# Gathering six experts' rows while the last two compute, and placing the last two's rows by one-hot products

## The chip, the cores and the metric

The kernel runs on one core of a Trainium2 chip. The metric is device time in microseconds (us) of one execution, the median of several runs. A TensorE clock of 1.0 in the profile is 2.4 GHz, one of 0.5 is 1.2 GHz.

The engines are named as in the profile: PE (matrix products; PEld is its weight load), DVE (VectorE), ACT (ScalarE), POOL (GpSimd), SP (issues most DMAs). A name with a q behind it (PEldq, DVEq, SPq) is an engine's instruction queue.

## The reference, cut to what matters

A two-layer network over 512 image tokens and 256 context tokens, width 1024. Each layer is a token mixer (two linear-attention scans) and a channel mixer, each followed by a layer norm. The second layer's channel mixer is a mixture of eight experts, of which each token uses two; behind it comes the last layer norm, whose output is the kernel's.

```python
def _moe_swiglu(h, router_w, router_b, w_gate_up, w_down):
    logits = (h @ router_w) + router_b
    top_val, top_idx = lax.top_k(logits, 2)
    combine = ... softmax(top_val) put at top_idx ...       # [512, 8]
    out = 0
    for e in range(8):
        gate, up = split(h @ w_gate_up[e], 2)               # 1024 x 2816
        out += combine[:, e] * ((silu(gate) * up) @ w_down[e])   # 1408 x 1024
# last layer, then the output:
x = _layer_norm(ALPHA * x + mod_x[:, 5] * f_x, ln_g[1, 1], ln_b[1, 1])
```

All inputs are float32; weights and activations are split in two parts (high and low, `wh`/`wl`), and a product is three matmuls (high by high, high by low, low by high).

## The kernel before

All that the change touches is the mixture of experts of the second layer (`moe_open`, `router_open`, `moe`), the last quarter of the run.

**Routing.** The experts are sorted by how many tokens chose them: rank 0 has the most. Rank r has room for `CAP[r]` tokens (256, 192, 192, 128, 128, 128, 64, 64). What does not fit goes to overflow blocks, computed in a loop after the streams (`For_i`, L1497) that runs as often as a table (`tabi`) says; in the profiled execution TensorE does no product in it. For each rank `index` finds the tokens in its slots (`ix`), and `gather_x` fetches their rows from DRAM with an indirect DMA on POOL.

**Streams.** Two streams run side by side, their steps interleaved by a cost table: ranks 0, 1, 2 and ranks 6, 3, 7, 4, 5 (`STREAMS`). Per expert 17.3 MB of weights are read by SP's DMAs in pieces of 0.5 MB into five raw buffers (`wr`), copied by ACT (`wh`, L134 and L149), subtracted by DVE (`wl`, L135 and L150), and multiplied on PE. So the last expert of the one stream is rank 2 (192 tokens, computed as 128 and 64) and that of the other rank 5 (128 tokens). At the third step of a stream's last expert `ahead` loads what the end needs: the residual rows `xr` (512 x 1024) and the norm's gain and bias `gb`.

**Rows back to tokens.** An expert's finished rows (`y`, weighted on DVE, L1434 and L1436) are written by SP to a DRAM table `ysd` with one row for each slot, plus 5 x 128 rows for overflow that are set to zero early (L1093). After the overflow loop POOL issues eight indirect DMAs (L1534) that read, for each of four tiles of 128 tokens and each of a token's two choices, the row at index `sidx` and add it to `xr[t]` while it lands.

**The end.** For each tile: moments on DVE (L833, L840), an inverse square root on POOL (L843), the affine on ACT (L1545), gain and bias on DVE and POOL (L1546, L1547), and the write of the output (L1548).

What sets the order: the code is written in program order, and a scheduler places each engine's instructions; the loop at L1497 is a barrier that nothing is moved across.

Of the kernel before, what the change touches and what calls it, by code (L numbers as in the profile page):

```python
# [7 lines left out]
F32 = mybir.dt.float32  # L8
F32R = mybir.dt.float32r
# [40 lines left out]
class Kern:  # L50
# [386 lines left out]
    def small(self, tag, n, parts=P, bufs=1):  # L437
        return self.sp.tile([parts, n], F32, tag=tag, name=self.nm(tag), bufs=bufs)
# [617 lines left out]
    def moe_open(self):  # L1056
        nc, I, tc = self.nc, self.I, self.tc
        self.rk_cm = tc.tile_pool(name="rk", bufs=1, side="right")
        rp = self.rp = self.rk_cm.__enter__()
        keep = lambda shape, tag, dt=F32: rp.tile([P] + list(shape), dt, name=tag)  # L1060
        self.xhd = tc.dram_tile([TX, D], F32, name="xhd")
        self.ysd = tc.dram_tile([NSLOT + NOVB * P, D], F32, name="ysd")
        self.bc5 = keep([D], "bc5")

        self.iota1 = keep([256], "iota1")
        nc.gpsimd.iota(self.iota1, pattern=[[1, 256]], base=1, channel_multiplier=0, allow_small_or_imprecise_dtypes=True)
        i8 = self.iota8
        self.caprow, self.ltm = keep([8], "caprow"), keep([8, 8], "ltm")
        for r in range(8):
            nc.gpsimd.memset(self.caprow[:, r:r + 1], float(CAP[r]))  # L1070
        nc.vector.tensor_tensor(self.ltm, i8[:, None, :].to_broadcast([P, 8, 8]), i8[:, :, None].to_broadcast([P, 8, 8]), OP.is_lt)
# [12 lines left out]
        self.rb = keep([N_E], "rb")  # L1084
        b = I["router_b"][0]
        nc.sync.dma_start(self.rb, bass.AP(tensor=b.tensor, offset=b.offset, ap=[[0, P], [1, N_E]]))

    def router_open(self):
        nc, lp = self.nc, self.lp
        zt = lp.tile([P, D], F32, name="zt")  # L1090
        nc.gpsimd.memset(zt, 0.0)
        for b in range(NOVB):
            nc.sync.dma_start(self.ysd[NSLOT + b * P:NSLOT + (b + 1) * P], zt)  # L1093
        self.full = lp.tile([P, KT, TX], F32, name="hfull")
        self.plog = self.psum("tr", [P, NX, N_E])

# [7 lines left out]
    def moe(self, l, aff):  # L1104
# [67 lines left out]
        def index(r, late=None):  # L1172

            for b in range((CAP[r] + P - 1) // P):
# [92 lines left out]
        nc.vector.tensor_tensor(c88, c88, bc(caprow), OP.mult)  # L1267
# [26 lines left out]
        nc.vector.tensor_tensor(sl, inc, bt(base), OP.add)  # L1294
        nc.vector.tensor_scalar(sl, sl, 1.0, None, op0=OP.subtract)

        alt = small([NX, 8], "alt")
        nc.vector.tensor_scalar(alt, ovp, float(NSLOT - 1), None, op0=OP.add)
        nc.vector.tensor_tensor(alt, alt, sl, OP.subtract)
# [139 lines left out]
        def rank_gen(r, xs, big):  # L1439
            e = bass.ds(nc.sync.value_load(expi[0:1, r:r + 1], min_val=0, max_val=7), 1)  # L1440
            gs = lambda i, j, c0, n: wgu[:, e, i:j, c0:c0 + n].rearrange("p e k c -> p (e k) c")
            ds_ = lambda a, n: wdn[:, e, a:a + n, :].rearrange("p e a c -> p (e a) c")
            off = sum(CAP[:r])

            def write(m, c, y):
                nc.sync.dma_start(ysd[off + m * P:off + m * P + y.shape[0], c], y)
            return expert(CAP[r], xs, gs, ds_, "accA" if big else "accB", write, lambda m: wsl[r, m])

        xr, gb = [], []

        def ahead(big):

# [28 lines left out]
        done, wait = [0, 0], None  # L1481
# [14 lines left out]
        novb = nc.values_load(tabi[0:1, 0:1], min_val=0, max_val=NOVB)  # L1496
        with tc.For_i(0, novb) as iv:  # L1497
            ev = nc.sync.value_load(tabi[0:1, bass.ds(iv + 1, 1)], min_val=0, max_val=7)
            o_h = mg.tile([P, NX, P], F32R, tag="gat", name="ovoh", bufs=3)
# [18 lines left out]
            xs, parts = gather_x(P, [ix])  # L1518
# [5 lines left out]
            ysv = ysd[NSLOT:, :].rearrange("(b p) c -> b p c", p=P)  # L1524

            def write(m, c, y):
                nc.sync.dma_start(ysv[bass.ds(iv, 1), :, c].rearrange("b p c -> (b p) c"), y)
            for _ in expert(P, xs, gs, ds_, "accB", write, lambda m: ow):
                pass


        for u in range(0, NX, 2):
            for j, t in itertools.product(range(2), (u, u + 1)):
                nc.gpsimd.indirect_dma_start(out=xr[t], out_offset=None, in_=ysd[:, :],  # L1534
                                             in_offset=bass.IndirectOffsetOnAxis(ap=sidx[:, j, t:t + 1].bitcast(mybir.dt.uint32), axis=0),
                                             compute_op=OP.add)
# [12 lines left out]
        fin_cm.__exit__(None, None, None)  # L1549
        mp_cm.__exit__(None, None, None)  # L1550
# [80 lines left out]
```

## Time and profile before

| | us |
|---|---|
| median of 3 runs | 2245.61 (2241.24 to 2247.71) |
| the profiled execution | 2239.29 |
| its span in the trace | 2237.4 |
| PE busy | 2063.8 (92%) |
| DVE busy | 1467.1 (66%) |
| POOL busy | 204.1 (9%) |
| last product of PE ends, from the span's start | 2189.8 |

The span is what the trace shows from the first to the last instruction; the execution's own time is 1.9 us longer. "Idle before, <- X" behind an instruction says how long its engine stood idle before it, and what ended the wait. Instructions that only wait, branch or issue DMAs are not counted as busy.

### The profile page before, as it was taken

How to read it: one execution, taken by the hardware profiler on the slowest of the kernel's cores; microseconds unless marked ns; L12 is line 12 of the kernel's file. 1: busy time of each engine (PE TensorE's matmuls, PEld its weight loads, DVE VectorE, ACT ScalarE, POOL GpSimd, SP SyncE). 2: the span in 40 equal slices, each digit the busy share in tenths (PEclk: the TensorE clock that was granted, in tenths of full speed). 3: DMA queues.
4: the chain of work that ended last, by engine and by line, in shares of the span. 5: the costliest groups of instructions: out<-in, count | busy, mean ns of one | idle time of the engine just before them, and what ended most of it. 6: DMA issues, size and time to landing. Idle time of an engine off the chain costs nothing. (4 is left out here: it accounts for less than half of the span.)

```text
span 2237.4 us, 31754 instructions
## 1 busy us (share of the span) xinstructions
PE 2063.8 (92%) x12273; PEld 1746.0 (78%) x12273; DVE 1467.1 (66%) x2519; ACT 891.3 (40%) x1411; POOL 204.1 (9%) x185
## 2 busy tenths in 40 slices
PE   8999699999999999999999999999768998889991
PEld 3887588986888888888888888898767787677771
DVE  4466584825787755555555677785688768677774
ACT  3346232323442222211224354334147656666661
POOL 1001101000200000022000011102510000000003
PEclk9999799999999999999999999999769999899995
DMA  7123112136454433322131221216278879788875
GB/s 257 48 82 109 37 36 83 46 139 221 156 185 148 157 132 132 132 76 76 60 120 44 81 71 43 67 57 211 101 229 283 257 262 309 236 278 294 287 268 129
DMA packets 233475, 332.29 MB, mean 149 GB/s; under 512 B 13936, under 2 KB 181044, under 8 KB 233320
## 3 DMA queue, kind: packets, MB, share of 16 engines
q1 hardware_dynamic: 229624, 318.09, 43.4%
q0 software_dynamic: 3696, 12.13, 2.1%
q8 instruction: 98, 1.61, 0.3%
q14 instruction: 57, 0.47, 0.1%
HBM read 305.98 MB, written 24.19 MB: 148 GB/s over the span
## 5 line engine op out<-in xcount | busy, mean ns | idle before, releaser
L165 PE MATMUL g<-xh,wh 128*128 128x512 f32 (+1 forms) x1168 | 400.8, 343 | 1.4 <-ACT xh L383 1.4
L166 PE MATMUL g<-xl,wh 128*128 128x512 f32 (+1 forms) x1168 | 400.2, 343 | 1.5 <-DVE xl L384 1.5
L167 PE MATMUL g<-xh,wl 128*128 128x512 f32 (+1 forms) x1168 | 400.0, 343 | 1.1 <-DVE wl L135 1.1
L135 DVE TENSOR_TENSOR wl<-wr,wh 128x1024 fp32r<-128x1024 f32 x240 | 295.6, 1241 | 158.3 <-ACT wh L134 157.4
L134 ACT ACTIVATE wh<-wr 128x1024 fp32r<-128x1024 f32 x240 | 249.4, 1055 | 257.9 <-PE sc L167 82.2
L165 PE MATMUL g<-wh,xh 128*128 128x256 f32 x1024 | 295.3, 289 | 13.5 <-DVE pre L979 5.3
L166 PE MATMUL g<-wl,xh 128*128 128x256 f32 x1024 | 294.9, 288 | 3.5 <-DVE wl L131 3.5
L167 PE MATMUL g<-wh,xl 128*128 128x256 f32 x1024 | 293.3, 287 | 0.0
L165 PEld LDWEIGHTS g<-xh,wh 128*128 128x128 f32 x1168 | 220.3, 189 | 29.9 <-issue 1.7
L166 PEld LDWEIGHTS g<-xl,wh 128*128 128x128 f32 x1168 | 220.2, 189 | 28.4 <-DVE xl L384 1.9
L167 PEld LDWEIGHTS g<-xh,wl 128*128 128x128 f32 x1168 | 220.3, 189 | 28.1 <-DVE wl L135 1.6
L150 DVE TENSOR_TENSOR wl<-wr,wh 128x1024 fp32r<-128x1024 f32 x154 | 185.6, 1219 | 50.6 <-ACT wh L149 49.0
L165 PEld LDWEIGHTS g<-wh,xh 128*128 128x128 f32 x1024 | 195.3, 191 | 19.5 <-DVE pre L979 3.8
L166 PEld LDWEIGHTS g<-wl,xh 128*128 128x128 f32 x1024 | 195.2, 191 | 5.9 <-DVE wl L131 5.3
L167 PEld LDWEIGHTS g<-wh,xl 128*128 128x128 f32 x1024 | 195.3, 191 | 0.0
L149 ACT ACTIVATE wh<-wr 128x1024 fp32r<-128x1024 f32 x154 | 160.3, 1055 | 62.9 <-DMA wr<-in_moe_w_gate_up 44.3
L866 DVE TENSOR_TENSOR s<-g,s 128x512 f32<-128x512 f32 (+1 forms) x44 | 24.4, 554 | 124.6 <-PE g L167 124.6
L523 POOL TENSOR_TENSOR ss<-ss,mhalf 128x4 f32<-128x4 f32 (+1 forms) x22 | 27.2, 1240 | 694.6 <-DVE ss L522 525.3
L466 PE MATMUL sc<-tmp,s 128*128 128x128 f32 x560 | 80.0, 291 | 4.1 <-DVE tmp L474 3.1
L466 PEld LDWEIGHTS sc<-tmp,s 128*128 128x128 f32 x560 | 71.6, 193 | 10.8 <-issue 4.4
L867 ACT ACTIVATE hh<-s 128x512 fp32r<-128x512 f32 (+1 forms) x44 | 23.1, 525 | 141.9 <-DVE s L866 141.9
L461 ACT ACTIVATE s<-slot 128x768 f32<-128x768 f32 (+1 forms) x56 | 44.4, 793 | 82.1 <-DVE slot L472 81.3
(483 smaller groups left out, 4083.0 us busy)
## 6 DMA issues: line engine op xcount, KB each, us to landing
wr<-in_moe_w_gate_up SPq DMA_DIRECT2D x176, 512.0 KB
wr<-in_moe_w_down SPq DMA_DIRECT2D x88, 512.0 KB
wr<-in_w_in SPq DMA_DIRECT2D x64, 512.0 KB
wr<-in_ffn_w_gate_up SPq DMA_DIRECT2D x44, 512.0 KB
wh<-in_w_ada SPq DMA_DIRECT2D x20, 1024.0 KB
wl<-in_w_ada SPq DMA_DIRECT2D x20, 1024.0 KB
wr<-in_ffn_w_down SPq DMA_DIRECT2D x22, 512.0 KB
wr<-in_w_ada SPq DMA_DIRECT2D x16, 512.0 KB
```

Source lines behind the costliest of these rows:

```text
L134: nc.scalar.activation(fl(h), r, AF.Copy)
L135: nc.vector.tensor_tensor(fl(lo), r, fl(h).bitcast(F32), OP.subtract)
L149: nc.scalar.activation(v(h, u), r, AF.Copy)
L150: nc.vector.tensor_tensor(v(lo, u), r, v(h, u).bitcast(F32), OP.subtract)
L165: nc.tensor.matmul(out, ah, bh, start=(i == 0), stop=False)
L166: nc.tensor.matmul(out, ah, bl, start=False, stop=False)
L167: nc.tensor.matmul(out, al, bh, start=False, stop=(i == n - 1))
L461: nc.scalar.activation(apx(kc, 0, [[2 * hh, qn // (2 * hh)], [hh, 2], [1, hh]]), apx(ka, 0, [[2 * hh, qn // (2 * hh)], [hh + T, 2], [1, hh ...
L466: nc.tensor.matmul(pl[:, c - a], kc[:, c * P:(c + 1) * P], apx(qa, c * P + T, [[2 * hh, 64 // hh], [hh - T, 2], [1, hh]]), start=True, sto ...
L523: nc.gpsimd.tensor_tensor(ss[:, :n], ss[:, :n], self.mhalf[:, :n], OP.pow)
L866: nc.vector.tensor_tensor(s, pu, s, OP.mult)
L867: nc.scalar.activation(hh[:, b, t0:t0 + n], s, AF.Copy)
```

## The change

- `ysd` holds rows for the slots of six ranks only, and one row of zeros (`NROW`). The last ranks of the two streams, `LAST` = (2, 5), have no rows there, and neither has the overflow; a token's choice that falls on one of these is given the index of the zero row.
- The eight indirect DMAs that add rows to `xr` (`ends`, L1475) are written right after `ahead` of rank 2 has run and rank 5 has begun, and no longer behind the loop.
- Rank 2 and rank 5 keep their rows in SBUF: `keep_y` copies each block of `y` as a high part on ACT (L1464) and a low part on DVE (L1465) into a tile `ys`.
- `onehot` compares a row of 0..511 (written by POOL, L1480) with each slot's token, which gives a matrix slots x 512 for each of the three blocks (128 and 64 slots of rank 2, 128 of rank 5).
- Behind the loop 48 matmuls of 512 columns (for each tile and half: three blocks, high and low) bring these rows to their tokens, and DVE adds the product to `xr` and sums the row (L1594).
- The last norm is written anew: the mean from the row sums, the squared distance on ACT (L1599), the inverse root on POOL (L1601), and two steps on DVE (L1602, L1605).
- The loop's overflow block takes its own buffers and adds its rows by one-hot products too.

```diff
-        self.ysd = tc.dram_tile([NSLOT + NOVB * P, D], F32, name="ysd")
+        self.ysd = tc.dram_tile([NROW + 1, D], F32, name="ysd")
...
-        zt = lp.tile([P, D], F32, name="zt")
+        zt = lp.tile([1, D], F32, name="zt")
...
-        for b in range(NOVB):
-            nc.sync.dma_start(self.ysd[NSLOT + b * P:NSLOT + (b + 1) * P], zt)
+        nc.sync.dma_start(self.ysd[NROW:NROW + 1], zt)
...
             def write(m, c, y):
+                if r in LAST:
+                    keep_y(ys[r], m, c, y)
+                    return
                 nc.sync.dma_start(ysd[off + m * P:off + m * P + y.shape[0], c], y)
...
+        def keep_y(yt, m, c, y):
+            n = y.shape[0]
+            nc.scalar.activation(yt[:n, m, 0, c], y, AF.Copy)
+            nc.vector.tensor_tensor(yt[:n, m, 1, c], y, yt[:n, m, 0, c].bitcast(F32), OP.subtract)
...
+        def onehot(o, io, ixf):
+            nc.vector.tensor_scalar(o, io, ixf, None, op0=OP.is_equal)
...
+        def ends():
+            for u in range(0, NX, 2):
+                for j, t in itertools.product(range(2), (u, u + 1)):
+                    nc.gpsimd.indirect_dma_start(out=xr[t], ..., in_=ysd[:, :], ..., compute_op=OP.add)
+            a, b = (mg.tile([P, 2, TX], F32R, tag="gat", ...) for _ in range(2))
+            io = mg.tile([P, TX], F32, tag="gat", ...)
+            nc.gpsimd.iota(io, pattern=[[1, TX]], ...)
+            ...
+                onehot(o[:n], io[:n], gidxf[r, m])
...
+            if places is None and all(started) and xr:
+                places = ends()
...
-        for u in range(0, NX, 2):
-            for j, t in itertools.product(range(2), (u, u + 1)):
-                nc.gpsimd.indirect_dma_start(out=xr[t], ..., in_=ysd[:, :], ..., compute_op=OP.add)
         for t in range(NX):
             f = xr[t]
-            o = fp.tile([P, D], F32, tag="o", name=self.nm("o"), bufs=4)
-            mean, r = self.moments(self.stats(f))
-            nb = fp.tile([P, 1], F32, tag="nb", name=self.nm("nb"), bufs=2)
-            nc.vector.scalar_tensor_tensor(nb, mean, -1.0, r, op0=OP.mult, op1=OP.mult)
+            sm = fp.tile([P, 2], F32, tag="sm", name=self.nm("sm"), bufs=2)
             for h in range(2):
                 c = slice(512 * h, 512 * h + 512)
-                nc.scalar.activation(o[:, c], f[:, c], AF.Identity, scale=r, bias=nb)
-                nc.vector.tensor_tensor(o[:, c], o[:, c], gb[0][:, c], OP.mult)
-                (nc.vector if h else nc.gpsimd).tensor_tensor(o[:, c], o[:, c], gb[1][:, c], OP.add)
+                p = self.psum("gu", [P, 512])
+                for i, (r, m, o) in enumerate(places):
+                    for j in range(2):
+                        nc.tensor.matmul(p, o[:, t * P:(t + 1) * P], ys[r][:o.shape[0], m, j, c], ...)
+                nc.vector.scalar_tensor_tensor(f[:, c], f[:, c], 1.0, p, op0=OP.mult, op1=OP.add, accum_out=sm[:, h:h + 1])
+            ...
+            nc.vector.tensor_scalar(nm, sm[:, 0:1], sm[:, 1:2], -1.0 / D, op0=OP.add, op1=OP.mult)
+            nc.scalar.activation(o, f, AF.Square, bias=nm, accum_out=r)
+            nc.vector.tensor_scalar(r, r, 1.0 / D, LN_EPS, op0=OP.mult, op1=OP.add)
+            nc.gpsimd.tensor_tensor(r, r, self.mhalf[:, 0:1], OP.pow)
+            nc.vector.scalar_tensor_tensor(f, f, nm, gb[0], op0=OP.add, op1=OP.mult)
+            for h in range(2):
+                c = slice(512 * h, 512 * h + 512)
+                nc.vector.scalar_tensor_tensor(o[:, c], f[:, c], r, gb[1][:, c], op0=OP.mult, op1=OP.add)
                 nc.sync.dma_start(self.out[0][t * P:(t + 1) * P, c], o[:, c])
```

What moves in the order of the instructions is seen at three places. The first is POOL's queue around the overflow loop, before: the gathers of `xrows` (this is `xr`) stand behind the loop's last branch.

```order
L1496 TENSOR_LOAD tabi
L1497 COMPARE_AND_BRANCH
L1497 ISA
L1497 UNCONDITIONAL_BRANCH
L1497 ISA
L1497 UNCONDITIONAL_BRANCH
L1627 BRANCH_PREFETCH_HINT
L1215 DMA gat_19085<-xhd,ovix 128x1024
L1497 REGISTER_ALU
L1497 COMPARE_AND_BRANCH
L1497 UNCONDITIONAL_BRANCH
L1534 DMA xrows<-ysd,sidx 128x1024 x7
```

The same queue now, from the gather of rank 5's input rows (`gat_17508`) on:

```order
L1219 DMA gat_17508<-xhd,ix_0_14303 128x1024
L1480 IOTA gat_18241 128x512
L1475 DMA xrows<-ysd,sidx 128x1024 x8
L1537 TENSOR_LOAD tabi
L1538 COMPARE_AND_BRANCH
```

All eight gathers stand ahead of the loop, and the row of 0..511 (`IOTA`) ahead of them.

The second place is DVE at the end of the streams, before. The `y` rows 18881 to 18892 are rank 2's, 19001 and 19004 rank 5's; `hs` and `hT` are rank 5's last hidden block, and the `wl` rows split its last weights.

```order
L1433 TENSOR_TENSOR y_18887<-sc_17688,y_18887 64x512
L135 TENSOR_TENSOR wl_18964<-wr_18969,wh_18963 128x1024
L1434 SCALAR_TENSOR_TENSOR y_18887<-y_18887,ws_1_14254,bc_13224 64x512
L1393 TENSOR_TENSOR hT_18778<-tr_18919,hT_18778 128x2x128
L1433 TENSOR_TENSOR y_18892<-o_17689,y_18892 64x512
L135 TENSOR_TENSOR wl_18990<-wr_18991,wh_18989 128x1024
L1434 SCALAR_TENSOR_TENSOR y_18892<-y_18892,ws_1_14254,bc_13224 64x512
L1325 TENSOR_TENSOR hs_18960<-g_18935,hs_18960 128x128
L1393 TENSOR_TENSOR hT_18924<-tr_18985,hT_18924 128x128
```

And now:

```order
L1440 TENSOR_TENSOR y_18920<-sc_17702,y_18920 64x512
L1465 TENSOR_TENSOR ys_17970<-y_18912,ys_17970 128x512
L1465 TENSOR_TENSOR ys_17970<-y_18916,ys_17970 128x512
L1441 SCALAR_TENSOR_TENSOR y_18920<-y_18920,ws_1_14263,bc_13224 64x512
L1440 TENSOR_TENSOR y_18926<-o_17703,y_18926 64x512
L1400 TENSOR_TENSOR hT_18809<-tr_18954,hT_18809 128x2x128
L1465 TENSOR_TENSOR ys_17970<-y_18920,ys_17970 64x512
L1441 SCALAR_TENSOR_TENSOR y_18926<-y_18926,ws_1_14263,bc_13224 64x512
L1332 TENSOR_TENSOR hs_18995<-g_18970,hs_18995 128x128
L135 TENSOR_TENSOR wl_18999<-wr_19004,wh_18998 128x1024
L1465 TENSOR_TENSOR ys_17970<-y_18926,ys_17970 64x512
L1400 TENSOR_TENSOR hT_18959<-tr_19020,hT_18959 128x128
```

The four `ys` rows of rank 2 are new, and both splits of the last weights have moved behind `hs`; the very last one (`wl_19025`) stands behind the last `hT`.

The third place is DVE behind the loop, before (the first rows):

```order
L833 BN_STATS st_19563<-xrows 128x6 x2
L840 BN_AGGR mv_19566<-st_19563 128x2
L842 TENSOR_SCALAR r_19568<-mv_19566 128x1
L833 BN_STATS st_19582<-xrows 128x6 x2
L840 BN_AGGR mv_19585<-st_19582 128x2
L1542 SCALAR_TENSOR_TENSOR nb_19571<-mv_19566,r_19568 128x1
L842 TENSOR_SCALAR r_19587<-mv_19585 128x1
L1546 TENSOR_TENSOR o_19562<-o_19562,gbrows 128x512 x2
```

and now:

```order
L1465 TENSOR_TENSOR ys_18513<-y_19040,ys_18513 128x512
L1594 SCALAR_TENSOR_TENSOR xrows,sm_19632<-xrows,g_19633 128x512
L1594 SCALAR_TENSOR_TENSOR xrows,sm_19632<-xrows,tr_19641 128x512
L1597 TENSOR_SCALAR nm_19650<-sm_19632 128x1
L1594 SCALAR_TENSOR_TENSOR xrows,sm_19661<-xrows,g_19662 128x512
L1600 TENSOR_SCALAR r_19652<-r_19652 128x1
L1602 SCALAR_TENSOR_TENSOR xrows<-xrows,nm_19650,gbrows 128x1024
L1594 SCALAR_TENSOR_TENSOR xrows,sm_19661<-xrows,tr_19670 128x512
L1605 SCALAR_TENSOR_TENSOR o_19649<-xrows,r_19652,gbrows 128x512 x2
```

Where DVE waited for a gathered tile, it now waits for two products (`g`, `tr`) and, at `r`, for ACT's sum of squares.

## Rows read from the trace of the kernel before

**Rows 1.** Chain that ended last, in order of time: start us, us, what.

```profile
2194.94 0.83 issue
2195.78 1.59 POOL xrows L1534
...
2216.10 6.57 DMA xrows<-ysd,sidx
...
2222.69 0.69 DVE st L833
...
2232.41 1.63 DVE o L1547
```

**Rows 2.** Stretches: start:end, us, busy of PE, PEld, DVE, ACT, POOL, PEclk, DMA share, GB/s.

```profile
2093.00:2173.00 80.00, 78.25 (x363) 62.81 (x362) 59.71 (x69) 50.96 (x67) 0.00 (x0) 1.00 0.85 285
2195.00:2205.00 10.00, 0.00 (x0) 0.00 (x0) 0.00 (x0) 0.00 (x0) 6.23 (x5) 0.50 0.74 129
```

**Rows 3.** Timeline of the streams' end: start us, us, engine, line, operation [idle before <-releaser].

```profile
2180.53 1.21 DVE L135 TENSOR_TENSOR wl<-wr,wh 128x1024 fp32r<-128x1024 f32 x1
2183.71 1.21 DVE L135 TENSOR_TENSOR wl<-wr,wh 128x1024 fp32r<-128x1024 f32 x1
2185.50 0.28 DVE L1325 TENSOR_TENSOR hs<-g,hs 128x128 f32<-128x128 f32 x1
2188.12 0.29 DVE L1393 TENSOR_TENSOR hT<-tr,hT 128x128 fp32r<-128x128 f32 x1 [2.35 <-ACT hT L1392]
2188.48 0.40 PE L1412 MATMUL g<-wl,hT 128*128 128x512 f32 x1
2189.14 1.44 DVE L1436 SCALAR_TENSOR_TENSOR y<-g,ws,bc 128x512 f32<-128x512 f32 x2 [0.73 <-PE g L1413]
2189.40 0.40 PE L1413 MATMUL g<-wh,hT 128*128 128x512 f32 x1
```

**Rows 4.** Line L1497 (the loop), PE's queue, 2189 to 2190.5 and 2195.1 to 2196.2 us.

```profile
L1497 PEldq COMPARE_BRANCH  x2: 97/2052/4007, 2189.9 to 2190.2; - x2
...
L1497 PEldq COMPARE_BRANCH  x1: 193/193/193, 2195.6 to 2195.6; - x1
```

**Rows 5.** DMA queues, 2195 to 2223 and 2093 to 2173 us: packets, MB, share of 16 engines.

```profile
q0 software_dynamic: 1152, 4.19, 81.7%
...
q1 hardware_dynamic: 19043, 22.76, 85.0%
```

**Rows 6.** Timeline of SP's queue, 2000 to 2190 us: issues of residual rows, rank 4's rows, last weights.

```profile
2016.53 0.37 SPq L1455 DMA_DIRECT2D xrows<-xd  x1
...
2089.76 1.04 SPq L1446 DMA_DIRECT2D ysd<-y  x2
...
2169.84 3.14 SPq L124 DMA_DIRECT2D wr<-in_moe_w_down  x3
```

**Rows 7.** Groups of instructions by form: busy us, mean ns of one.

```profile
L329 DVE SCALAR_TENSOR_TENSOR acc<-wl,cond,acc 128x1024 f32<-128x1024 f32 x40 | 50.5, 1280 | 8.5 <-DMA wl<-in_w_ada 8.0
L1393 DVE TENSOR_TENSOR hT<-tr,hT 128x256 fp32r<-128x256 f32 x20 | 8.3, 415 | 0.8 <-ACT hT L1392 0.7
L1546 DVE TENSOR_TENSOR o<-o,gbrows 128x512 f32<-128x512 f32 x8 | 5.3, 685 | 1.1 <-ACT o L1545 1.1
L781 DVE TENSOR_SCALAR slot<-slot,om 128x512 f32<-128x512 f32 x8 | 3.8, 481 | 1.0 <-ACT slot L777 1.0
L1545 ACT ACTIVATE o<-xrows,nb,r 128x512 f32<-128x512 f32 x8 | 6.0, 803 | 36.1 <-DMA xrows<-ysd,sidx 26.9 <-DVE nb L1542 9.3
```

**Rows 8.** PE's timeline where the clock rises, at the experts' start; 256 columns each.

```profile
1657.36 0.41 PE L165 MATMUL tr<-xs,wh 128*128 128x256 f32 x1
1657.58 0.41 PE L166 MATMUL tr<-xs,wh 128*128 128x256 f32 x1
...
1659.65 0.28 PE L165 MATMUL tr<-xs,wh 128*128 128x256 f32 x1
1659.76 0.28 PE L166 MATMUL tr<-xs,wh 128*128 128x256 f32 x1
```

**Rows 9.** Stretches around an earlier fall of the clock, columns as in rows 2.

```profile
1575.00:1580.00 5.00, 3.37 (x11) 2.45 (x11) 4.98 (x5) 0.00 (x0) 4.84 (x5) 0.50 0.00 0
1580.00:1585.00 5.00, 5.00 (x27) 5.00 (x27) 3.58 (x6) 0.00 (x0) 2.63 (x3) 0.58 0.00 0
1585.00:1590.00 5.00, 5.00 (x45) 5.00 (x44) 2.63 (x6) 0.00 (x0) 0.00 (x0) 1.00 0.26 105
```

**Rows 10.** Timeline of SP and ACT, 1547 to 1572 us: zero rows issued, weights copied.

```profile
1547.80 7.74 SPq L1093 DMA_DIRECT2D ysd<-zt  x5
...
1570.15 1.71 ACT L130 ACTIVATE wh<-wr,col 128x256 fp32r<-128x256 f32 x4 [0.77 <-DMA wr<-in_w_out]
```

More of the change, by code (lines that the diff above doesn't have):

```diff
@@ L1067, in moe_open @@
         i8 = self.iota8
-        self.caprow, self.ltm = keep([8], "caprow"), keep([8, 8], "ltm")
+        self.caprow, self.rowrow, self.ltm = keep([8], "caprow"), keep([8], "rowrow"), keep([8, 8], "ltm")
         for r in range(8):
             nc.gpsimd.memset(self.caprow[:, r:r + 1], float(CAP[r]))
+            nc.gpsimd.memset(self.rowrow[:, r:r + 1], float(CAP[r] if r not in LAST else 0))
         nc.vector.tensor_tensor(self.ltm, i8[:, None, :].to_broadcast([P, 8, 8]), i8[:, :, None].to_broadcast([P, 8, 8]), OP.is_lt)
@@ L1191, in index @@
                 gidx[r, b] = ix
+                if r in LAST:
+                    xf = gidxf[r, b] = rp.tile([n, 1], F32, name=f"ixf{r}_{b}")
+                    nc.vector.tensor_copy(xf, pi[:, 0:1])
                 if late is None:
@@ L1295, in moe @@
         nc.vector.tensor_scalar(sl, sl, 1.0, None, op0=OP.subtract)
+        lst = small([8], "lst")
+        nc.vector.tensor_scalar(lst, rank, float(LAST[0]), None, op0=OP.is_equal)
+        nc.vector.scalar_tensor_tensor(lst, rank, float(LAST[1]), lst, op0=OP.is_equal, op1=OP.add)
         alt = small([NX, 8], "alt")
-        nc.vector.tensor_scalar(alt, ovp, float(NSLOT - 1), None, op0=OP.add)
-        nc.vector.tensor_tensor(alt, alt, sl, OP.subtract)
+        nc.vector.tensor_tensor(ins_, ins_, bt(lst), OP.max)
+        nc.vector.tensor_scalar(alt, sl, -1.0, float(NROW), op0=OP.mult, op1=OP.add)
         nc.vector.tensor_tensor(alt, alt, ins_, OP.mult)
@@ L1442, in rank_gen @@
             ds_ = lambda a, n: wdn[:, e, a:a + n, :].rearrange("p e a c -> p (e a) c")
-            off = sum(CAP[:r])
+            off = sum(CAP[q] for q in range(r) if q not in LAST)
             def write(m, c, y):
+                if r in LAST:
+                    keep_y(ys[r], m, c, y)
+                    return
                 nc.sync.dma_start(ysd[off + m * P:off + m * P + y.shape[0], c], y)
             return expert(CAP[r], xs, gs, ds_, "accA" if big else "accB", write, lambda m: wsl[r, m])
-        xr, gb = [], []
+        xr, gb, ys = [], [], {}
+        def keep_y(yt, m, c, y):
[7 more added lines that the diff above has]
+                for j, t in itertools.product(range(2), (u, u + 1)):
+                    nc.gpsimd.indirect_dma_start(out=xr[t], out_offset=None, in_=ysd[:, :],
+                                                 in_offset=bass.IndirectOffsetOnAxis(ap=sidx[:, j, t:t + 1].bitcast(mybir.dt.uint32), axis=0),
+                                                 compute_op=OP.add)
+            a, b = (mg.tile([P, 2, TX], F32R, tag="gat", name=self.nm("gat"), bufs=3) for _ in range(2))
+            io = mg.tile([P, TX], F32, tag="gat", name=self.nm("gat"), bufs=3)
+            nc.gpsimd.iota(io, pattern=[[1, TX]], base=0, channel_multiplier=0, allow_small_or_imprecise_dtypes=True)
+            out = []
+            for (r, m), o in zip([(r, m) for r in LAST for m in range((CAP[r] + P - 1) // P)], (a[:, 0], a[:, 1], b[:, 0])):
+                n = min(P, CAP[r] - m * P)
+                onehot(o[:n], io[:n], gidxf[r, m])
+                out.append((r, m, o[:n]))
+            return out
         def ahead(big):
@@ L1469, in stream @@
                         ahead(big)
+                        ys[r] = mg.tile([P, 2 if big else 1, 2, D], F32R, tag="xsA" if big else "xsB", name=self.nm("ys"), bufs=2)
                     elif step == PREP:
@@ L1480, in moe @@
         gens = [stream(STREAMS[0], True), stream(STREAMS[1], False)]
-        done, wait = [0, 0], None
+        done, wait, started, places = [0, 0], None, [False, False], None
         while gens[0] or gens[1]:
@@ L1498, in moe @@
             ev = nc.sync.value_load(tabi[0:1, bass.ds(iv + 1, 1)], min_val=0, max_val=7)
-            o_h = mg.tile([P, NX, P], F32R, tag="gat", name="ovoh", bufs=3)
+            o_h = fp.tile([P, NX, P], F32R, name="ovoh")
             o_t = mp.tile([P, 512], F32, tag="xf", name="ovt2", bufs=2)[:, :P]
@@ L1517, in moe @@
             nc.vector.tensor_copy(ix, pi[:, 0:1])
-            xs, parts = gather_x(P, [ix])
+            ixf = mp.tile([P, 1], F32, name="ovixf")
+            nc.vector.tensor_copy(ixf, pi[:, 0:1])
+            xs, parts = gather_x(P, [ix], at=fp.tile([P, 2 * KT * P], F32R, name="ovx"))
             for f in parts:
@@ L1523, in moe @@
             ds_ = lambda a, n: wdn[:, e, a:a + n, :].rearrange("p e a c -> p (e a) c")
-            ysv = ysd[NSLOT:, :].rearrange("(b p) c -> b p c", p=P)
-            def write(m, c, y):
-                nc.sync.dma_start(ysv[bass.ds(iv, 1), :, c].rearrange("b p c -> (b p) c"), y)
+            yt = fp.tile([P, 1, 2, D], F32R, name="ovy")
+            io = fp.tile([P, TX], F32, name="ovio")
+            nc.gpsimd.iota(io, pattern=[[1, TX]], base=0, channel_multiplier=0, allow_small_or_imprecise_dtypes=True)
@@ L1528, in moe @@
+            ot = fp.tile([P, TX], F32R, name="ovot")
+            onehot(ot, io, ixf)
+            def write(m, c, y):
+                keep_y(yt, 0, c, y)
+                for t in range(NX):
+                    p = self.psum("sc", [P, 512])
+                    for i in range(2):
+                        nc.tensor.matmul(p, ot[:, t * P:(t + 1) * P], yt[:, 0, i, c], start=i == 0, stop=i == 1)
+                    nc.vector.tensor_tensor(xr[t][:, c], xr[t][:, c], p, OP.add)
             for _ in expert(P, xs, gs, ds_, "accB", write, lambda m: ow):
@@ L1543, in moe @@
             for h in range(2):
                 c = slice(512 * h, 512 * h + 512)
-                nc.scalar.activation(o[:, c], f[:, c], AF.Identity, scale=r, bias=nb)
-                nc.vector.tensor_tensor(o[:, c], o[:, c], gb[0][:, c], OP.mult)
-                (nc.vector if h else nc.gpsimd).tensor_tensor(o[:, c], o[:, c], gb[1][:, c], OP.add)
+                p = self.psum("gu", [P, 512])
+                for i, (r, m, o) in enumerate(places):
+                    for j in range(2):
+                        nc.tensor.matmul(p, o[:, t * P:(t + 1) * P], ys[r][:o.shape[0], m, j, c],
+                                         start=i + j == 0, stop=(i == len(places) - 1 and j == 1))
@@ new lines, in moe @@
+                nc.vector.scalar_tensor_tensor(f[:, c], f[:, c], 1.0, p, op0=OP.mult, op1=OP.add, accum_out=sm[:, h:h + 1])
+            o = fp.tile([P, D], F32, tag="o", name=self.nm("o"), bufs=4)
+            nm = fp.tile([P, 1], F32, tag="nm", name=self.nm("nm"), bufs=2)
+            nc.vector.tensor_scalar(nm, sm[:, 0:1], sm[:, 1:2], -1.0 / D, op0=OP.add, op1=OP.mult)
+            r = fp.tile([P, 1], F32, tag="r", name=self.nm("r"), bufs=2)
+            nc.scalar.activation(o, f, AF.Square, bias=nm, accum_out=r)
@@ L1600 @@
 STREAMS = ((0, 1, 2), (6, 3, 7, 4, 5))
+LAST = tuple(s[-1] for s in STREAMS)
 LEAD = 0.95
@@ L1603 @@
 CAP = (256, 192, 192, 128, 128, 128, 64, 64)
-NSLOT = sum(CAP)
+NROW = sum(c for r, c in enumerate(CAP) if r not in LAST)
 NYG = 8
```

8 lines of the change are left out of this document (3 added, 5 removed).

## The prediction

> **What bounds the kernel now.** I read the chain of waits first, at its end. After the streams nothing computes: the chain runs over "issue", one gather's descriptors on POOL (1.59 us), the gathers' flight (the last step shown 6.57 us) and the last tile's norm on DVE, which ends at 2234.04 [rows 1]. Then I read the stretches: from 2093 to 2173 PE is busy 78.25 of 80 us at a granted clock of 1.00, with DVE at 59.71, ACT at 50.96 and the 16 DMA engines at 0.85; in 2195 to 2205 PE is idle, the clock 0.50, and the DMA engines still 0.74 busy [rows 2]. So two stages have different limits: PE with DMA close behind it while weights stream, and the gathers' DMA time behind the loop. The change moves work from the second to the first. Then the streams' last ten us, one instruction at a time [rows 3], and the loop, which PE's queue enters with a branch of 4.0 us and leaves at 2195.8 [rows 4].
>
> The sum is made against the profiled execution, 2239.3 us (span 2237.4 and 1.9). The median is 6.3 us above it; I carry the difference over to the median. About 0.3% (6.7 us) is what a measurement of this kernel can tell from no change.
>
> **The tail: a gain.** Before, PE's last product ends at 2189.40 + 0.40 = 2189.8 [rows 3], the span at 2237.4: 47.6 us. After:
> - the loop stays, whose passage ends at 2195.8 [rows 4]: 6.0 us;
> - the gap called "issue" behind it, 0.8 [rows 1];
> - the first half tile's six products. At half clock 256 columns start every 0.22 us, at full clock every 0.11 [rows 8], so 512 columns take 0.43 or 0.23 (estimates). The clock stands at 0.50 there [rows 2]: 6 x 0.43 = 2.6;
> - DVE: eight adds out of PSUM at 0.72, as the `y` rows of 128x512 take (1.44 for two) [rows 3] = 5.8; four `L1602` at 1.28, by the nearest form of 128x1024 [rows 7] = 5.1; eight `L1605` at 0.72 = 5.8; eight one-column steps, taken at 0.15, half of a 128x128 row [rows 3] = 1.2. Together 17.9. DVE waits for the second product (2.6 against its 0.7), so about 2 more; the square sum on ACT (2 x 0.80 [rows 7]) lies beside the next tile's adds. 20;
> - from DVE's last end, 2234.0 [rows 1], to the span's end 2237.4, the output's write: 3.4.
>
> 6.0 + 0.8 + 2.6 + 20 + 3.4 = 32.8, a gain of 14.8. What decides inside it is the clock: at an earlier fall it stood at 0.50, 0.58 and 1.00 in three successive stretches of 5 us, the last two with PE busy throughout [rows 9]. If it comes back so, PE (six products in 1.4 us) is ahead of DVE (2.2 per half). If it doesn't, the 48 products take 48 x 0.43 = 20.6, and behind them stands the last tile's own chain (add, square, root, two steps, about 6.5): 6.0 + 0.8 + 20.6 + 6.5 + 3.4 = 37.3, 4.5 worse. Full clock from the start would be about 3 better.
>
> **The gathers beside the weights: a loss.** They now wait for rank 4's rows, whose writes are issued at 2089.76 (the residual rows were loaded long before, 2016.53) [rows 6]. So they run from about 2093. Behind them on POOL stands nothing until the loop; POOL is idle there [rows 2], and the one-hots' IOTA stands ahead of them. Alone, their 1152 packets (4.19 MB) keep 16 engines busy for 81.7% of 28 us = 22.9 us; in the 80 us of the stage the weights' queue takes 85.0%, which leaves 12.0 [rows 5]. Short by 10.9. The weights have a little room at the end: the last split ends at 2184.92 and the last product that needs it starts at 2188.48 [rows 3]; some 3.2 us of it is free. 10.9 - 3.2 = 7.7 us that PE waits. Bounds: if the gathers cost only their bytes, 4.19 MB at the weights' 285 GB/s [rows 2] = 14.7, less 12.0 and the room, the loss is nil. If they shut the weights out, it is 22.9, since nothing that PE has lost comes back while DMA is at 85%. I take the middle value, from packet times, as the gathers' packets (3.6 KB each) were timed on this same path.
>
> **The order at the streams' end: a small loss.** Before, both last splits `wl` (1.21 each) were done by 2184.92, ahead of `hs` at 2185.50, and `hT` at 2188.12 waited for ACT [rows 3]. Now the first of them stands behind `hs` and the other behind `hT`, with four `ys` subtractions of about 0.7 each (as `o` of 128x512, 685 ns [rows 7]) among them. PE's products with `wl` then wait for 1.2 us of DVE and its start, and the `ys` rows push `hs` by some of their 2.8 where DVE has no slack. I take 2.5, between 0 (the products by `wh` fill it) and 3.5.
>
> **Small edits.** Five DMAs of zero rows go (7.74 us of SP's time) and one remains; ACT waited 0.77 for weights shortly after [rows 10]. I take -0.8; a shift of SP's queue there could give -3 to +1. Three one-hots of 128x512 at 0.48 [rows 7] fall into DVE's 20 idle us of 80 [rows 2]; if that cover is gone they cost 1.4. The `keep_y` copies on ACT (0.8 each [rows 7]) replace writes to DRAM, and ACT is idle 29 us of 80. The small copies, memsets and index steps of the routing: 0, between 0 and 1.
>
> **The sum.** -14.8 + 7.7 + 2.5 - 0.8 = -5.4. Profiled execution about 2234; median 2245.6 - 5.4 = 2240. The change breaks even when PE loses 7.7 + 5.4 = 13.1 us to the gathers.
>
> **The rivals.**
>
> A, the forecast: gathers that cost PE about 8 us. Its own range, over the middle half of the bounds, is -10 to -1: 2235.6 to 2244.6. Chance 0.43.
>
> B, the gathers fit. For it: the 12 us of idle DMA, five raw buffers that let weights be read ahead, and that two tiles of rows in flight need no fixed time, as nothing waits for them until the loop. Against it: the stage's 0.85. PE then loses about 0.5: -14.8 + 0.5 + 2.5 - 0.8 = -12.6, 2233. Chance 0.29.
>
> C, the weights' queue loses its turns, and the kernel gets slower. Place: 2093 to about 2130. Both queues share the 16 engines. Should they take equal bytes while both have work, the gathers' 22.9 us and the weights' 4.19 MB, at 68 us for 22.76 MB [rows 5] = 12.5 us, fill 35.4 us, in which PE gets what it eats in 14.7 (at 285 GB/s). It loses 20.7, if it has no lead when they start: -14.8 + 20.7 + 2.5 - 0.8 = +7.6, 2253. It decides from 13.1 us of loss on. For it: PE's 78.25 of 80 shows that weights come just in time. Against it: five buffers of lead, and eight gathers that can't all be in flight, as the two on a tile add to the same rows. Chance 0.17.
>
> The Trainium skill has a rule for this, in "DMA: Bandwidth & Descriptors", section "Queues, rings and completion order": each engine goes round-robin between the queues it has work for, a whole packet at a time. Taken with this trace's mean packets of 3.6 KB for the gathers and 1.2 KB for the weights, turn about, 1.4 MB of weights would pass beside the gathers, in some 27 us; PE would lose 22, and the time would be about 2254, next to C. No stretch of this trace has such gathers beside weights at 0.85, so no row decides it.
>
> D, the clock stays at 0.50 through the tail: 4.5 worse than A, 2245 (no change). For it: PE has been idle some 6 us when its products start, and waits for DVE between them. Against it: [rows 9]. Chance 0.08.
>
> E, the change doesn't do what it says: a wait holds the gathers on POOL until near the loop, for instance a late `sidx` or `xr`. They would then end no earlier than before by much, and the products come on top: 2246 to 2248. Against it: `xr` is loaded from 2016.53 [rows 6], and the order has the gathers ahead of the loop. Chance 0.03.
>
> **How the numbers follow.** The likeliest is A, 2240. Faster by over 0.3% means below 2238.9: all of B (0.29) and the lower part of A (0.11) = 0.40. Within 0.3%: the rest of A (0.32), D (0.07), a part of C (0.04) and of E (0.01) = 0.44. Slower, above 2252.3: C (0.13), E (0.02), D (0.01) = 0.16. The range reaches from 2230 (B with a tail 3 better) to 2254 (C): it leaves out about 2 in 10, above a loss of 22 us and below a gain of 15.
>
> **What would show it.** In 2093 to 2173: DMA share near 1.0 until the gathers have landed, and PE's busy time 8 us below 78.25 (B: 77 or more, C: about 58). PE's last product of the streams at 2189.8 + 7.7 + 2.5 - 0.8, about 2199 (B 2192, C 2212). From it to the span's end 33 us; 37 with a clock of 0.50 throughout (D). DVE's rows of L1594 near 0.72, L1602 near 1.28, L1605 near 0.72; the first L1594 some 9 us behind the streams' last product. On POOL the gathers issued from about 2093 (E: behind 2150). I am wrong if the gathers beside weights cost much less than their packet times alone (B) or much more (C), or if the passage of the loop takes longer than 6.0 us now that its overflow block holds products of its own.

## The result, and the profile after

The changed kernel takes 2254.04 us (median of 19 runs, 2246.76 to 2263.99), the kernel before beside it 2240.61 (19 runs): a ratio of 1.0061, with a 95% interval of 1.0049 to 1.0073. It is 13 us slower. I had forecast 5 us faster.

The profiled executions differ by more (spans 2260.3 and 2237.4), so I cut them at two events that each trace has: the issue of rank 4's last row write, from which the gathers can run, and the end of the streams' last product. Before, these stand at 2090.5 (the second of the two writes in [rows 6]) and 2189.8 [rows 3]; after, at 2096.0 and 2218.0. The **stage** between them grew from 99.3 to 122.0 us (+22.7), the **tail** behind shrank from 47.6 to 42.3 (-5.3). The two events after (SP's and PE's timelines; the second of the two writes starts 0.7 us behind the first):

```profile
2095.30 1.03 SPq L1456 DMA_DIRECT2D ysd<-y  x2
...
2217.62 0.40 PE L1420 MATMUL g<-wh,hT 128*128 128x512 f32 x1
```

What lies ahead of the first event differs by 5.5 us; in the thirteen profiles of this study that event stands anywhere from 2084.7 to 2096.0, so I read nothing out of it.

The stage, in stretches of 20 us (columns as in [rows 2]):

```profile
2093.00:2113.00 20.00, 17.77 (x79) 13.55 (x77) 11.37 (x13) 8.97 (x12) 7.67 (x5) 1.00 0.88 238
2113.00:2133.00 20.00, 10.97 (x35) 8.54 (x35) 5.77 (x7) 4.74 (x7) 6.31 (x4) 0.66 1.07 258
2133.00:2153.00 20.00, 13.90 (x49) 10.98 (x49) 12.79 (x14) 11.98 (x15) 0.00 (x0) 0.83 0.78 263
2153.00:2173.00 20.00, 20.00 (x90) 16.03 (x89) 11.94 (x15) 10.82 (x15) 0.00 (x0) 1.00 0.73 241
```

PE is busy 62.6 of these 80 us; it was 78.25 in [rows 2]. POOL issues the first gather at 2099, its first packets move at 2105, and the last gather has landed at 2134. In between the DMA engines are full (1.07 in 2113 to 2133, by the packets' durations), and ACT, which copies each weight tile as it lands, waits for them. Its timeline (columns as in [rows 3]):

```profile
2106.44 0.39 ACT L1331 ACTIVATE hs<-g 128x256 f32<-128x256 f32 x1
2112.79 1.06 ACT L149 ACTIVATE wh<-wr 128x1024 fp32r<-128x1024 f32 x1 [5.96 <-DMA wr<-in_moe_w_gate_up]
2119.33 1.06 ACT L149 ACTIVATE wh<-wr 128x1024 fp32r<-128x1024 f32 x1 [5.48 <-DMA wr<-in_moe_w_gate_up]
2120.29 0.37 ACT L1399 ACTIVATE hT<-tr 128x256 fp32r<-128x256 f32 x1
...
2128.70 1.06 ACT L149 ACTIVATE wh<-wr 128x1024 fp32r<-128x1024 f32 x1 [7.60 <-DMA wr<-in_moe_w_gate_up]
```

And PE's timeline in the same stretch:

```profile
2122.03 0.80 PE L1376 MATMUL tr<-wh,xs 128*128 128x512 f32 x1 [11.27 <-DVE hT L1400]
2122.62 0.63 PE L1377 MATMUL tr<-wl,xs 128*128 128x512 f32 x1
2123.05 0.63 PE L1378 MATMUL tr<-wh,xs 128*128 128x512 f32 x1
...
2139.26 0.80 PE L1376 MATMUL tr<-wh,xs 128*128 128x512 f32 x1 [6.09 <-DVE hs L1332]
```

A weight tile of 0.5 MB lands every 6.5 to 9.4 us. PE waits 11.3 and 6.1 us, and behind each wait its products of 512 columns start every 0.43 us for some 6 us (14 products in each place), 0.2 more each than at full clock: another 6 us. 11.3 + 6.1 + 6 = 23, the stage's loss. What is named as the end of both waits is not a weight tile but `hT` and `hs`, which ACT and DVE write behind weight copies in their queues (2120.29 above); how much of the waits is due to this order, and not to the late weights themselves, no run separates. The queues in 10 us of the burst (packets, MB, share of 16 engines) (2110 to 2120) show who had the engines:

```profile
q0 software_dynamic: 467, 1.72, 85.9%
q1 hardware_dynamic: 617, 0.61, 21.0%
```

The tail begins with PE's products of `L1592`; its timeline, six products in a row:

```profile
2223.75 3.52 PE L1592 MATMUL g<-ys,gat 128*128 128x512 f32 x6 [5.73 <-DVE ys L1465]
2227.07 3.35 PE L1592 MATMUL tr<-ys,gat 128*128 128x512 f32 x6
2230.22 3.35 PE L1592 MATMUL g<-ys,gat 128*128 128x512 f32 x6
```

Stretches of 5 us of the tail, for the clock (columns as in [rows 2]):

```profile
2220.00:2225.00 5.00, 1.25 (x3) 0.61 (x3) 0.69 (x1) 0.00 (x0) 0.00 (x0) 0.53 0.02 5
2225.00:2230.00 5.00, 5.00 (x10) 2.76 (x11) 0.70 (x2) 0.00 (x0) 0.00 (x0) 0.50 0.00 0
2240.00:2245.00 5.00, 5.00 (x11) 2.20 (x10) 1.31 (x4) 0.19 (x2) 0.00 (x0) 0.50 0.09 35
2245.00:2250.00 5.00, 4.34 (x9) 2.12 (x8) 3.46 (x8) 1.24 (x2) 1.52 (x1) 0.50 0.00 0
```

The clock stays at 0.50 to the last product, and six products start in 3.15 us, not in the 2.6 of 6 x 0.43. The timeline of the weight loads (PEld) tells where the rest goes:

```profile
2223.75 0.50 PEld L1592 LDWEIGHTS g<-ys,gat 128*128 128x128 f32 x2 [6.17 <-issue]
2224.90 0.50 PEld L1592 LDWEIGHTS g<-ys,gat 64*128 64x128 f32 x2 [0.65 <-issue]
2226.05 0.50 PEld L1592 LDWEIGHTS g<-ys,gat 128*128 128x128 f32 x2 [0.65 <-issue]
2226.64 0.76 PEld L1592 LDWEIGHTS tr<-ys,gat 128*128 128x128 f32 x2
```

Two loads of a block come together, the next block's only after 1.15 us, 0.29 more than the two products need (0.86). It is so on both sides of the 64-row block; from one half's last block to the next half's first, both of 128 rows, there is no such gap (2226.05 to 2226.64).

### The profile page after: what moved, and what is told of

Its sections match the earlier page's. It is cut to its first block, busy times and chain, and to the rows that moved or that the text cites. A ratio compares the mean times of both kernels' runs of the same rounds, so it can differ in the third digit from the quotient of the medians.

```text
span 2260.3 us, 31875 instructions
## 1 busy us (share of the span) xinstructions
PE 2101.3 (93%) x12321; PEld 1767.1 (78%) x12321; DVE 1472.0 (65%) x2537; ACT 894.0 (40%) x1417; POOL 206.6 (9%) x190
## 5 line engine op out<-in xcount | busy, mean ns | idle before, releaser
L1376 PE MATMUL tr<-wh,xs 128*128 128x512 f32 (+1 forms) x144 | 61.4, 426 | 24.5 <-DVE hT L1400 15.4
L466 PEld LDWEIGHTS sc<-tmp,s 128*128 128x128 f32 x560 | 71.3, 192 | 11.6 <-issue 5.3
```

Of the source, the lines that this page charges most:

```text
L466: nc.tensor.matmul(pl[:, c - a], kc[:, c * P:(c + 1) * P], apx(qa, c * P + T, [[2 * hh, 64 // hh], [hh - T, 2], [1, hh]]), start=True, sto ...
L1376: nc.tensor.matmul(q, x[:, 0, k], h, start=st, stop=False)
```

## The experiments

Theories: **T1**, the gathers take the DMA engines from the weights; **T2**, the cost is in the streams' new order and copies; **T3**, the tail's products are slow for the 64-row block and the clock. Ratios are to the kernel before, run beside each; stage and tail are cut in each run's trace as above. A ratio stands on several executions, a stage and a tail on the one that was profiled; by the ratios the changes against the kernel before differ from the last column by up to 6 us.

| | ratio (95%) | stage | tail | both, less 146.9 |
|---|---|---|---|---|
| before | 1 | 99.3 | 47.6 | 0 |
| changed | 1.0061 (1.0049 to 1.0073) | 122.0 | 42.3 | +17.4 |
| e1_no_gathers | 0.9964 (0.9950 to 0.9977) | 102.2 | 42.4 | -2.3 |
| e2_late | 0.9981 (0.9967 to 0.9994) | 99.0 | 45.0 | -2.9 |
| e3_full_block | 1.0010 (0.9992 to 1.0028) | 119.7 | 31.6 | +4.4 |
| e5_spread | 1.0038 (1.0020 to 1.0055) | 114.5 | 42.3 | +9.9 |
| e8_quarter_rows | 1.0042 (1.0026 to 1.0058) | 112.1 | 41.3 | +6.5 |
| e10_plain_gathers | 1.0002 (0.9987 to 1.0018) | 108.4 | 42.6 | +4.1 |
| e9_one_switch | 1.0019 (1.0002 to 1.0035) | 121.5 | 35.3 | +9.9 |
| e4_late_full | 0.9960 (0.9946 to 0.9975) | 99.2 | 39.7 | -8.0 |
| e6_late_order | 0.9971 (0.9958 to 0.9985) | 99.6 | 36.2 | -11.1 |
| e7_early | 0.9977 (0.9966 to 0.9988) | 98.7 | 44.6 | -3.6 |
| e11_best | 0.9935 (0.9911 to 0.9959) | 100.5 | 35.4 | -11.0 |

**e1_no_gathers** deletes the loop over `indirect_dma_start` in `ends`.

> Leaves out the eight gathers: the rows of the six other experts are missing from the output; the order of the other engines' instructions is that of the changed kernel. Theory (the gathers hold back the weights): the weights' stage loses nothing, the streams' last product comes 47 us before the old span's end again, and the time is 2254 - 22 = about 2232 (2228 to 2237). Rival (the order of the last splits and the new copies beside the streams cost it): the streams still end late, 2245 or more.

The stage is 102.2 and the ratio 0.9964: 22 us of 2241 below the changed kernel. T2 falls: its order, copies and one-hots are all still there. (The 2.9 us above 99.3 are one wait of 2.0 us, which ends at 2115.45, and eight products at half pace behind it; e2, with the same order, doesn't have them.)

**e2_late** writes the indices of four gathers into a tile `si` only after the last raw weight tile has landed, and leaves the other four behind the loop:

```diff
+                nc.gpsimd.tensor_copy(si[0:1, ...], self.rl[0:1, 0:1])
+                nc.gpsimd.tensor_copy(si[:, ...], sidx[:, j, t:t + 1])
+        rows([(j, t) for j in range(2) for t in range(2)], si)
...
+        rows([(j, t) for j in range(2) for t in range(2, NX)], None)
```

> The gathers of the first two tiles start when the last weights have landed, those of the other two behind the loop. Theory (the gathers cost only where they meet the weights): no loss in the stage; tail about 42 as in the changed kernel, perhaps 2 more where a tile's rows are late: 2232 to 2238. Rival (the gathers' 23 us of DMA time must be paid wherever they stand): 2245 to 2254.

The first gather on POOL, and PE's last product of the streams:

```profile
2178.30 1.61 POOL L1477 DMA_INDIRECT xrows<-ysd,si  x1 [0.57 <-POOL si L1474]
...
2187.52 0.39 PE L1420 MATMUL g<-wh,hT 128*128 128x512 f32 x1
```

The stage is 99.0, that of the kernel before; all eight gathers are made, and no us of it is lost. T1 holds. This version is faster than the kernel before, by 4 us.

**e5_spread** gates each gather in the same way, five raw tiles apart. **e10_plain_gathers** drops `compute_op=OP.add`. **e8_quarter_rows** reads four rows of 256 columns for each row of 1024.

> The eight gathers are held apart: each waits for the fifth raw weight tile after the one before, so they go through the whole stage one at a time. Theory (a burst of gathers takes more turns than the weights' lead covers): the loss falls from 22 us to the shortfall of DMA time, 8 to 11: 2241 to 2244. Rival (the sum of DMA time decides and the turns do not matter, or each gather alone stops PE): 2251 to 2257.

> The eight gathers write the rows instead of adding them, so the residual and the first of a token's two rows are missing from the output; number, size and place of the gathers and all else stay. Theory (an engine is held by each gathered packet for as long as the packet takes, and a packet that adds takes about twice as long): the stage's loss falls from some 20 us to about 10, 2244. Rival (the number of turns or the bytes decide, not how long a packet takes): 2252 to 2256.

> Gathers placed as in the changed kernel, each cut into four of 256 columns, so that a packet is at most 1 KB instead of 4. Theory (the DMA engines go between the two queues packet by packet): while both have work, the weights get about as many bytes as the gathers, not a third as in the changed kernel (0.61 against 1.72 MB in 10 us), and the longest wait of TensorE for weights falls from 11 us to below 6. Rival (each queue gets its share of bytes or time whatever its packets): the shares stay, the wait too.

Spread out, the gathers still cost 15 us of the stage (by the ratio 8.5 us above the kernel before, 2249 on the scale of 2240.6, where I had expected 2241 to 2244). So the burst is about a third of the loss (7.5 of 22.7). Of the 15.2 that are left PE's waits are 9.6 (11.6 us in e5's stage, 2.0 before); the other some 5 us go with four stretches of 10 us in which the granted clock is 0.72 to 0.97. I put this rest down to the sum of DMA time, of which the stage has too little left. That each gather alone stops PE, the rival, is not excluded: 2249 lies between the two ranges, and the gathers came unevenly, 4 to 20 us apart. Plain gathers cost 9. The queues of e10 in 10 us of the burst (2105 to 2115; packets, MB, share):

```profile
q0 software_dynamic: 625, 2.30, 59.8%
q1 hardware_dynamic: 1526, 1.52, 44.5%
```

A gathered packet that adds holds its engine 85.9% of 160 us / 467 = 0.29 us, a plain one 59.8% of 160 / 625 = 0.15. With the price of a packet halved the loss went from 22.7 to 9.1, at the same bytes. It is not gone, though the plain gathers' DMA time, 1152 x 0.153 / 16 = 11.0 us (an estimate), is less than the 12.0 idle before. The quarter rows were a poor test of the turns: POOL issues one every 2.1 us on average, so I take it that the queue was often empty, and put down to that that the weights got four to five times the gathers' bytes (2.45 to 2.75 MB against 0.55 to 0.64 in each 10 us from 2105 to 2145). The longest wait fell to 2.5 us as expected, but for another reason, and the stage still lost 12.8 to the same bytes cut into more packets. That the engines alternate by packet fits the changed kernel's 467 to 617; with 625 to 1526 in e10 I can't tell it from an empty queue, and it stays open. The rule of the Trainium skill ("DMA: Bandwidth & Descriptors", "Queues, rings and completion order") is a turn of a whole packet for each queue, which it puts at about 9 to 17 descriptors; whether the packets that the profile counts are these, no run here shows.

**e3_full_block** fills rank 2's second block up to 128 rows of zeros; **e9_one_switch** orders the blocks 128, 128, 64 and in the other half 64, 128, 128.

```diff
+                if n < P:
+                    nc.vector.tensor_scalar(o[n:], io[n:], -1.0, None, op0=OP.is_equal)
+                    nc.gpsimd.memset(ys[r][n:, m].bitcast(F32), 0.0)
...
-                out.append((r, m, o[:n]))
+                out.append((r, m, o))
```

> The block of 64 slots is filled up with zeros to 128 rows. Theory (the change between 128 and 64 rows empties TensorE's pipe, 0.29 us twice per half tile): six products take 2.58 us rather than 3.15, 4.6 us less in all, 2249; if the clock rises with it, up to 8 us more, 2241. Rival (the longer pitch has another cause): 2254, the six products still 3.15.

> The changed kernel with another order of the three blocks: 128, 128, 64 rows in the first half of a tile and 64, 128, 128 in the second, so that TensorE changes between 128 and 64 rows once in a half tile instead of twice. Theory (each change costs 0.29 us): six products take 2.87 us instead of 3.15, 2.3 us less in all, about 2252; the clock then shows whether these gaps or the half-filled block keep it at 0.50: 2252 if it stays, 2243 if it comes back as with the filled block. Rival (the cost is that of the 64-row products themselves): 3.15 and 2254 again.

PE's timeline in e3, where the first six products start in 2.73 us and the later ones in half of it:

```profile
2218.97 2.93 PE L1595 MATMUL g<-ys,gat 128*128 128x512 f32 x6 [6.04 <-DVE ys L1465]
2221.70 1.89 PE L1595 MATMUL tr<-ys,gat 128*128 128x512 f32 x6
2223.43 1.53 PE L1595 MATMUL g<-ys,gat 128*128 128x512 f32 x6
```

The stretches of e3's tail show the clock back at 1.00 from 2224 on:

```profile
2218.00:2221.00 3.00, 2.02 (x5) 1.64 (x6) 0.16 (x1) 0.00 (x0) 0.00 (x0) 0.50 0.02 5
2221.00:2224.00 3.00, 3.00 (x12) 2.40 (x11) 1.07 (x3) 0.00 (x0) 0.00 (x0) 0.76 0.00 0
2224.00:2229.00 5.00, 5.00 (x24) 4.02 (x23) 4.35 (x11) 1.24 (x2) 1.54 (x1) 1.00 0.00 0
```

The tail falls to 31.6, with more rows computed than before, not fewer. In e9 the loads show one gap in six products and the half takes 2.85 us (PE's timeline):

```profile
2220.51 3.06 PE L1592 MATMUL tr<-ys,gat 64*128 64x512 f32 x6
2223.36 3.06 PE L1592 MATMUL g<-ys,gat 128*128 128x512 f32 x6
```

The clock comes back too, later (0.50 in 2220 to 2225, 0.85 in 2225 to 2230). So the gap belongs to the change of rows, 0.29 us each time, and with fewer gaps the clock came back sooner: by the stretches' mean clock 3.5 to 5.2 us after the first product in the five profiles with a filled block, 9 in e9. It isn't the gaps alone: with both gaps in each half the clock rose 18 to 19 us after the first product in e8 and e2, and not at all in the changed kernel, e1, e5 and e10. What tells these apart stays open. The Trainium skill ("TensorEngine Tiling (Array Packing)", "Key Properties") says that changing the tiling mode drains TensorE; the trace agrees in that the gap stands only where the rows change, but that it is such a drain no run shows.

**e4, e6, e7, e11** join late gathers and the filled block and move the gathers about the loop: four ahead and four behind (e4), five and three (e6), all ahead from the fourth-last raw tile on (e7), six and two from the fifth-last on, with a single copy of the indices (e11). The copies of e7 and e11 had hardly been made when the last weights landed, so both are late gathers too.

> Late gathers and the filled block together. Theory (the two gains are of different stages, but the rows of the last two tiles now come last): of the 14 us that the filled block gave beside early gathers some 6 remain, since the second pair of gathers is issued only behind the loop and lands some 18 us later: 2226 to 2230. Rival (they add up fully): 2220. Rival (the late rows become the bound entirely): 2233, as without the filled block.

> As the run before, with five gathers ahead of the loop (first rows of all four tiles, second rows of the first) and three behind it, so that no gather behind the loop waits for another. Theory (the late rows bound the tail): the last rows land about 5 us sooner and the time is 3 to 5 us below that of the run before, 2222 to 2226. Rival (POOL comes later to the loop and holds it): same or slower.

> Filled block; all eight gathers ahead of the loop, from the fourth-last raw weight tile on, the first rows of all tiles first. Theory (a packet of the gathers takes the turn of a packet of weights): three or four weight tiles of 0.5 MB are slowed by some 6 us each beside four gathers, of which the lead covers a part: the streams end 3 to 8 us later than with late gathers, but no row is waited for behind the loop: 2222 to 2230. Rival (POOL holds the loop because of the second rows): 2230 or more.

> Filled block; six gathers ahead of the loop, held until the fifth-last raw weight tile has landed, with one copy of the indices in place of eight; two gathers behind the loop. Theory (POOL's last issue before the loop sets the loop's passage, and four gathers beside the last weights cost nothing): POOL is through by the time of the last product, the loop is left 2 to 3 us sooner than with the last weights awaited, 2222 to 2226. Rival (the gathers reach the last weights and the streams end later): 2228 or more.

In e4 DVE waits for the last tiles' rows (1.52 us) and POOL's inverse root stands behind a gather. In e6 the waits for rows are 0.75 and 0.28 us and the tail is 3.5 shorter, though the ratios of e4 and e6 don't differ beyond their intervals. e7 shows the price of the barrier (its timelines: POOL's last gather, then PE's first product of the tail):

```profile
2189.62 1.55 POOL L1477 DMA_INDIRECT xrows<-ysd,si  x1 [0.49 <-issue]
...
2201.64 2.93 PE L1605 MATMUL g<-ys,gat 128*128 128x512 f32 x6 [18.23 <-issue]
```

PE was done at 2183.4, but POOL comes to the loop 8 us later, and everyone leaves it 10 us after POOL. What these 10 us wait for is the gathers' flight: one wait of POOL in the loop, from 2192.8 on, takes 7.4 us, and the last gather, issued at 2189.62, lands 10.5 us later, at 2200.1. In e6 the releaser is named (line of the loop in e7; DVE's timeline in e6):

```profile
L1551 POOLq EVENT_SEMAPHORE  x13: 17/43/7395, 2191.5 to 2201.0; - x13
...
2194.51 0.69 DVE L1465 TENSOR_TENSOR ys<-y,ys 128x512 fp32r<-128x512 f32 x1 [7.76 <-DMA xrows<-ysd,si]
```

In all five versions with late gathers PE's first product of the tail starts 1.0 to 1.5 us after the last gather ahead of the loop has landed (e2 2196.5, e4 2193.0, e6 2193.6, e7 2200.1, e11 2202.7), but 7.0 to 10.5 us after POOL has issued it. So the late gathers are not free: between PE's products lie 9.0 to 9.9 us (18.2 in e7), not the 5.7 of the changed kernel.

No time was lost in e7's stage (98.7), but the gathers did not meet the last weights, though I had expected it: POOL's copies of the indices took 5 us, and by then all weights had landed. What a few gathers beside the last weights cost is not known, and e11 doesn't show it either. e11 is the best by its ratio: 0.9935, some 15 us below the kernel before. Its interval overlaps those of e4 and e6, and its trace is no better than e6's; the loop is not left sooner, though I had expected it (9.8 us between PE's products, 9.6 in e6). On the scale of 2240.6 the ratios give 2232 (e4), 2234 (e6), 2235 (e7) and 2226 (e11); by them only e11 is within its range, at its edge.

## Why the prediction was wrong

**What bounds the kernel:** right. Two stages, and the change moves DMA work into the one that has little left.

**The tail** was mis-sized: -14.8 forecast, -5.3 measured. The passage of the loop took 5.7 where I had 6.8, DVE's steps 0.69, 1.27 and 0.70 where I had 0.72, 1.28 and 0.72, and the write at the end 3.4 as forecast. What failed is the clock. I let it come back as in [rows 9] and put its staying away at 0.08; it stayed away, and PE's 25.6 us of products set the tail. That alone was priced at 4.5 (the tail of 37.3 us, rival D). On top came a term that I had left out, 16 changes between 128 and 64 rows at 0.29: 4.6 us. I had rows for the 128-row products alone and took them for all. The two make up the 9.5 that are missing but for 0.4, and the rest of the sum stands: in e3, with no such changes and the clock back, the tail is 31.6 where I had 32.8.

**The gathers beside the weights**: +7.7 forecast, some 20 measured (22.7 in the profile of the changed kernel, 20.4 and 22.2 in those of e3 and e9). The failing step is the subtraction: 22.9 of DMA time less the 12.0 idle and 3.2 of lead. It would need the gathers to fall into the idle times. They came in a burst, three or four at once, and PE's lead lasted 6 us (first packets at 2105, PE stands from 2110.8). In 2105 to 2134 the weights' queue moved 3.22 MB beside the gathers' 4.19 MB. At the 285 GB/s of before PE eats that in 11.3 us, which leaves it an estimated 17.7 of the 29 us without weights; the two waits are 17.4. Even the plain gathers of e10, which by my subtraction fit into the idle 12.0, cost 9.1; e5, which spaces them out, still lost 15, 9.6 of it waits. The second thing that the sum left out is that PE's wait costs the clock: 6 of the 23 us are products at half speed behind the waits. The upper bound (22.9) is met in size only: the weights were not shut out. Rival C named the place and the order of the price (20.7); its equal bytes are not what the queues show, with 4.19 to 3.22 MB over the whole, and 2.8 times the weights' bytes (1.72 to 0.61) while both had work. That C's time (2253) meets 2254.04 is luck: its sum holds a tail gain of 14.8 where 5.3 came and no slow products, and starts from a median of 2245.6 where the kernel before measures 2240.61. The 2254 that the prediction works out by the rule of the Trainium skill ("DMA: Bandwidth & Descriptors", "Queues, rings and completion order") meets it by the same luck.

**The order at the streams' end**: +2.5 forecast, nothing measured. PE waited 0.29 us for a split at its end; e2, e4 and e7 have the same order, and their stages are 99.0, 99.2 and 98.7 against 99.3. **The zero rows** and the small edits can't be told from the scatter ahead of the stage.

So the sum had the signs of its two large terms right, and both sizes wrong in the same direction: the loss nearly three times, the gain a third.

## What to carry to other kernels

Count work that is moved under a stage that streams weights in the packets' own durations and not in bytes, and don't subtract the DMA engines' idle time from it unless it can fall there: this stage, at 0.85 of its DMA time, lost 22.7 us to 22.9 of gathers in a burst, 15 when they were spread, and 9 to plain ones that would have fitted. Put behind the last weights, some 80 us later, the same transfers cost the streams nothing, but the loop that is a barrier waited until those ahead of it had landed, 3 to 4 us longer than with none in flight. One-hot products with a part-filled block were cheaper filled up with zeros (a tail of 31.6 us and not 42.3).

## What was not expected of the hardware

- A gathered packet (3.7 KB on average) that adds to its target holds a DMA engine about 0.29 us, a plain one 0.15.
- The loop let the engines go only when the gathers issued ahead of it had landed: PE's next product came 1.0 to 1.5 us after that in five profiles.
- A change between products of 128 and of 64 rows costs TensorE 0.29 us at a granted clock of 0.50.
- TensorE can be busy for 25 us in the profile's sense, with two such gaps in every six products, while the granted clock stays at 0.50.
